# A transformer layer's feed-forward part: four sums per block move from GpSimd to VectorE and read PSUM, raw w2 tiles are fetched two slots ahead, and the last superblock keeps one chain per token tile

## The chip, the cores and the metric

One Trainium2 chip, of which the kernel uses one core. The metric is the device time in microseconds (us) of one execution. TensorE is called PE here, VectorE DVE, ScalarE ACT, GpSimd POOL, and SyncE, which issues nearly all DMAs, SP.

## What is computed

One layer of a transformer with a mixed attention: retention heads beside grouped-query attention, then a feed-forward part whose activation is the square of a relu. The sizes are 2048 tokens of width 1024, and 4096 hidden columns. All is float32 at the kernel's border.

```python
x = x + g1 * (jnp.concatenate([ret, att], axis=-1) @ w_out)

h2 = _modulate(_rmsnorm(x, norm2_g), sh2, sc2)
x = x + g2 * _sqrelu_mlp(h2, w_ff1, w_ff2)
...
def _sqrelu_mlp(h, w1, w2):
    return jnp.square(jax.nn.relu(h @ w1)) @ w2
...
return _rmsnorm(x, final_norm_g)
```

The change touches only the last two lines of the layer: the feed-forward part and its way to the end of the kernel.

## The kernel before, in words

**Number format.** Each float32 operand of a large product is split into two float16 parts, hi and lo. A product of 128 rows of depth then takes three matmuls of 512 columns: hi by hi, hi by lo, lo by hi. A split is two instructions: ACT writes hi as a float16 copy, and DVE subtracts hi from the source to give lo (L66 to L72, `split16`).

**Seven products for eight.** Both feed-forward products are done block-wise by a scheme with seven half-size products and some sums and differences (Strassen-Winograd). Up: a block `b` is 256 hidden columns for one half of the tokens (1024). There are 16 blocks for each half, 32 in all. The seven products of a block are listed in `UP` (L1643): each has a weight part (`a11`, `s1`, ...) made by `sum_w1` on POOL and `form_w1` on ACT and DVE, a part of the activations `hf`, and the name of its PSUM chain, A, B or C. Product n=0 starts chain A, n=1 chain B, n=3 chain C; the others go on accumulating in an open chain. After each product, `up_out` (L1673) takes what it needs from PSUM: ACT copies chain A to tile `v` after n=0, to `q` after n=2, to `w` after n=4 (L1687); DVE adds chain B to `v` after n=1 and chain C to `q` after n=6 (L1678), and chain C to `w` after n=4 (L1699); ACT applies the relu (L1682). So the four quarters of the hidden activations end up in four SBUF tiles: a11 in `v`, a12 in `r`, a21 in `q`, a22 in `w`. They are squared by ACT (L1708).

**The sums of u.** From the squared quarters `sum_r` makes, on POOL, s1 = a21 + a22, s3 = a11 - a21, s2 = s1 - a11, s4 = a12 - s2 (L1713). In the profile these are the four rows of L1713 whose outputs are `s`, `q`, `v` and `r`. The seven tiles a11, a12, a22, s1 to s4 are then split into float16 pairs by `split_r`: the profile calls them `ua` (of `v`, `r`, `w`) and `us` (of `s`, `v`, `q`, `r`).

**Down.** Two blocks make a superblock `s`; there are eight for each half of the tokens, 16 in all. Its seven products are listed in `DOWN` (L1749): each takes one of those seven pairs, one tile `w2t` of w2, and a chain A to D for each of four tiles `m` of 128 tokens (`down`, L1799; PSUM tiles `pd`, four banks). After each, `down_out` (L1813) adds the bank, scaled, to an SBUF tile on DVE (L1824): either to a quarter of an output tile `acc`, or, for n=0 and n=2, to `accu` ("u"), a running sum that three of the four output quarters share. At the end of a half, `add_sum` (L1826) adds `accu` to those three quarters.

**Order.** The instruction order on each engine is written by hand. A unit `g` is one step of the loop at L1972: the four parts of one up product (12 matmuls), `up_out`, and two down products of the superblock before (six matmuls each) with their `down_out`. A block takes 7 units, a superblock 14; there are 224 units, then a tail with the last superblock's 28 down products. Side work is put into units by `at(g, ...)`: the entries with `first=True` run between the first down product and its `down_out`, the others between the second and its own. `rows_of` (L1731) places squares, splits and sums. In units 4 to 13 there is no down product yet.

**Preparing w2.** During the first half of the tokens, 16 jobs (`w2_job`, L1754) each fetch two raw tiles `w2r` of w2, multiply them with a gate row on POOL (L1765), form four differences on POOL (L1551) and seven float16 pairs `w2f` on ACT and DVE (L71, L72), and store the pairs to DRAM. Each job has a slot of five units; fetch stands in the slot's unit 0, gate in 1, forms in 2 to 5. Between the jobs are four slots `h_pair`, which prepare the second half's activations (`hb`, `hs`, `hp`) in a similar way. Job 0 runs in the prelude, interleaved with the last of the attention (`prelude`, L1863); there, the places are counted from `k0`, the end of attention.

**PSUM.** Eight banks: four for up (`pu`, pool `ps1`, handed out in turn) and, from unit 14 on, four for down (`pd`, pool `ps2`).

Of the kernel before, what the change touches and what calls it, by code (L numbers as in the profile page):

```python
# [22 lines left out]
P = 128  # L23
# [32 lines left out]
def layer_kernel(ctx: ExitStack, tc: tile.TileContext, a: dict, out: bass.AP):  # L56
# [1548 lines left out]
    ff = {}  # L1605
# [3 lines left out]
    def open_early():  # L1609
        attn.close()  # L1610
        keep.close()
        ff["h"] = pool(early_ff, "fh", 7)
        ff["w1"] = pool(early_ff, "fw", 7)
        ff["r"] = pool(early_ff, "fr")
        ff["ps1"] = pool(early_ff, "fp1", 4, space=PSUM)

# [39 lines left out]
    pu, rs = {}, {}  # L1656

    def up_part(b, n, k):
        c = UP[n][2]
        first = n in (0, 1, 3)  # L1660
        if k == 0 and first:
            pu[c] = ff["ps1"].tile([P, HALF], F32, name="pu", tag="pu")
        whi, wlo = (w1[b, n][:, x, k] for x in range(2))
        hi, lo = (hs[n][:, x, k] for x in range(2))
        more = {"skip_group_check": not first}
        mm(pu[c], whi, hi, start=first and k == 0, stop=False, **more)  # L1666
        mm(pu[c], whi, lo, start=False, stop=False, **more)  # L1667
        mm(pu[c], wlo, hi, start=False, stop=k == 3, **more)  # L1668

    def new_r(name):  # L1670
        return ff["r"].tile([P, HALF], F32, name=name, tag="r", bufs=8)

    def up_out(b, n):  # L1673
# [6 lines left out]

        def relu(r, src=None):
            nc.scalar.activation(r, r if src is None else src, AF.Relu, scale=scu)  # L1682
            return r
# [5 lines left out]
        if n == 0:  # L1689
            copy("v")  # L1690
        elif n == 1:
            x["a11"] = relu(add(x["v"], x["v"]))
        elif n == 2:
            copy("q")
        elif n == 3:
            x["c"] = ps
        elif n == 4:
            copy("w")
            nc.vector.tensor_tensor(x["w"], x["c"], x["w"], op=ALU.add)  # L1699
            x["a22"] = relu(x["w"])  # L1700
        elif n == 5:
            x["a12"] = relu(new_r("r"), ps)
        elif n == 6:
            x["a21"] = relu(add(x["q"], x["q"]))

# [4 lines left out]
    def sum_r(b, to, x, y, op, at=None):  # L1710
        r = rs[b]
        r[to] = r[at] if at else new_r(to)
        nc.gpsimd.tensor_tensor(r[to], r[x], r[y], op=op)  # L1713

# [16 lines left out]
    def rows_of(b, g):  # L1731
# [5 lines left out]
        at(g + 7, split_r, b, "a12")  # L1737
        at(g + 7, square_r, b, "a21")
        at(g + 7, sum_r, b, "s1", "a21", "a22", ALU.add)
        at(g + 7, sum_r, b, "s3", "a11", "a21", ALU.subtract, "a21")  # L1740
        at(g + 8, sum_r, b, "s2", "s1", "a11", ALU.subtract, "a11")
        at(g + 8, sum_r, b, "s4", "a12", "s2", ALU.subtract, "a12")
        at(g + 8, split_r, b, "s1", first=True)
        at(g + 9, split_r, b, "s2", first=True)
# [9 lines left out]
    def w2_job(b, load, do):  # L1754
# [23 lines left out]
        for i in range(2):  # L1778
            load(0, fetch, i)
            do(1, gate, i)  # L1780
        plan = [(2, "b11"), (2, "b21"), (3, "t2"), (3, "t1"), (4, "b22"), (4, "t3"), (5, "t4")]
        for k, w in plan:
            do(k, form, w)
            load(k + 1, store, w)
        do(2, difference, x, "t1", "b12", "b11")
        do(2, difference, x, "t2", "b22", "t1")
        do(3, difference, x, "t3", "b22", "b12", "b12")
        do(4, difference, x, "t4", "b21", "t2", "t1")

# [7 lines left out]
    accs, pd, sums = [None] * NM, {}, {}  # L1797

    def down(s, n, m):  # L1799
        ua, _, c, _ = DOWN[n]  # L1800
        first = n in (0, 2, 3, 5)
        if first:
            pd[c, m] = ff["ps2"].tile([P, HALF], F32, name="pd", tag="pd")
# [59 lines left out]
    def prelude(k0):  # L1863
# [29 lines left out]
    with tc.manual_schedule():  # L1893
# [20 lines left out]
        for i, job in enumerate(jobs):  # L1914
# [47 lines left out]
        for lo, g0 in ((0, g + 9), (4, g + 13)):  # L1962
# [3 lines left out]
            for m in range(lo, lo + 4):  # L1966
# [130 lines left out]
```

## Time and profile before

| | us |
|---|---|
| time, median of 3 runs | 2908.1 (2907.28 to 2911.85) |
| time of the profiled execution | 2909.34 |
| span of that execution in the profile | 2907.6 |
| PE busy | 2674.7 (92%) |
| DVE busy | 2144.3 (74%) |
| ACT busy | 1569.5 (54%) |
| POOL busy | 1609.6 (55%) |

The profiled execution's time is 1.7 us longer than its span. The profile page gives busy time by engine, groups of instructions by line with the idle time in front of them and what ended it, and a chain of waits; the trace can be asked for groups, waits and the busy time in any stretch. The feed-forward matmuls start at 1578 us of the span, unit 14 (the first with down products) near 1680 us, and the last matmul ends near 2896 us. PEclk is the granted clock of the PE array as a share of full speed.

### The profile page before, as it was taken

The page shows a single profiled execution, that of the slowest core. Times are in us where ns is not written, and L with a number is a line of the kernel's source. Part 1 is how long each engine was busy: PE and PEld are TensorE (multiplying, and loading weights), DVE is VectorE, ACT ScalarE, POOL GpSimd, SP SyncE. Part 2 cuts the span into 40 slices and gives each one's busy share as a digit, 9 for nine tenths or more (in the row PEclk, how much of TensorE's full clock was granted, in tenths as well). Part 3 has the DMA queues.
Part 4 walks back from the last instruction along what each step waited for, and adds up shares of the span by engine and source line. Part 5 has one row for each costly group of instructions (what it writes and reads, how often), then busy time and mean ns, then how long its engine had stood idle before and what let it go on. Part 6 is the DMA issues. An engine that isn't in the chain of part 4 may idle for free.

```text
span 2907.6 us, 44941 instructions
## 1 busy us (share of the span) xinstructions
PE 2674.7 (92%) x16768; PEld 1423.5 (49%) x16768; DVE 2144.3 (74%) x3209; ACT 1569.5 (54%) x2711; POOL 1609.6 (55%) x1275
## 2 busy tenths in 40 slices
PE   7999999988899999999997689889889999999997
PEld 2545644545566666665664234334334444444443
DVE  4856777578877778777774788878798776666666
ACT  3634753247777777777775454444444454444433
POOL 2623762437666668677776766766664443333324
PEclk8999999999999999999999899999999999999999
DMA  7478667552112123232325555544555352222212
GB/s 251 132 254 298 203 203 228 173 187 76 41 61 85 50 82 91 73 97 72 100 62 210 184 175 181 167 151 161 170 169 190 113 195 80 80 80 80 80 51 94
DMA packets 267945, 394.64 MB, mean 136 GB/s; under 512 B 107143, under 2 KB 158343, under 8 KB 265934
## 3 DMA queue, kind: packets, MB, share of 16 engines
q1 hardware_dynamic: 267438, 390.72, 41.5%
q8 instruction: 132, 2.16, 0.3%
q10 hardware_dynamic: 288, 1.05, 0.1%
q14 instruction: 87, 0.71, 0.1%
HBM read 290.87 MB, written 100.82 MB: 135 GB/s over the span
## 4 chain that ended last, share of the span: by engine, by line
PE 61%; DVE 15%; POOL 6%; issue 6%; DMA 6%; ACT 5%; SPq 1%; POOLq 0%; DVEq 0%; ACTq 0%
PE pso L646 5%; PE pso L647 5%; PE pso L648 5%; PE pd L1809 4%; PE pd L1811 4%; PE pd L1810 4%; PE pu L1666 4%; PE pu L1668 4%; PE pu L1667 4%; PE o L239 3%; PE mp L168 3%; PE st L205 3%; PE st L206 3%; DVE w2f L72 2%; DVE plo L224 2%
## 5 line engine op out<-in xcount | busy, mean ns | idle before, releaser
L181 DVE TENSOR_REDUCE nm<-mp 128x1 f32<-128x512 f32 (+1 forms) x576 | 390.3, 685 | 155.0 <-PE mp L168 126.4
L222 POOL TENSOR_TENSOR plo<-p,phi 128x1024 f16<-128x1024 f32 x160 | 353.1, 2208 | 163.8 <-ACT phi L215 135.1
L211 ACT ACTIVATE p<-st 128x512 f32<-128x512 f32 x576 | 338.4, 598 | 180.8 <-PE st L206 108.6
L1666 PE MATMUL pu<-hf,w1f 128*128 128x512 f16 x896 | 346.2, 386 | 41.2 <-ACT w L1687 26.4
L1667 PE MATMUL pu<-hf,w1f 128*128 128x512 f16 x896 | 346.1, 386 | 0.0
L1668 PE MATMUL pu<-hf,w1f 128*128 128x512 f16 x896 | 345.5, 386 | 0.0
L215 ACT ACTIVATE phi<-p 128x1024 f16<-128x1024 f32 x288 | 304.3, 1057 | 0.0
L647 PE MATMUL pso<-wlo,h 128*128 128x512 f16 (+1 forms) x816 | 295.6, 362 | 2.8 <-DVE wlo L544 2.8
L646 PE MATMUL pso<-whi,h 128*128 128x512 f16 (+1 forms) x816 | 295.7, 362 | 1.1 <-ACT whi L543 1.1
L648 PE MATMUL pso<-whi,h 128*128 128x512 f16 (+1 forms) x816 | 295.4, 362 | 0.0
L1713 POOL TENSOR_TENSOR s<-q,w 128x512 f32<-128x512 f32 x32 | 43.3, 1355 | 453.4 <-ACT q L1708 453.4
L224 DVE TENSOR_TENSOR plo<-p,phi 128x512 f16<-128x512 f32 x256 | 243.4, 952 | 15.6 <-ACT phi L215 14.4
L238 PE MATMUL o<-wv,plo 128*128 128x65 f16 x2304 | 235.3, 193 | 18.4 <-POOL plo L222 9.8
L1824 DVE SCALAR_TENSOR_TENSOR acc<-pd,sc,acc 128x512 f32<-128x512 f32 x320 | 234.9, 742 | 11.5 <-PE pd L1811 10.8
L239 PE MATMUL o<-wv,phi 128*128 128x129 f16 x2304 | 243.0, 221 | 0.0
L238 PEld LDWEIGHTS <-plo 128*128 128x128 f16 x2304 | 206.1, 98 | 64.0 <-POOL plo L222 20.8
L1809 PE MATMUL pd<-w2t,us 128*128 128x512 f16 x512 | 196.0, 383 | 41.7 <-DVE acc L1824 39.7
L205 PE MATMUL st<-qr,ks 128*128 128x512 f16 x576 | 220.5, 383 | 14.8 <-ACT p L211 13.3
L206 PE MATMUL st<-qr,ks 128*128 128x512 f16 x576 | 220.7, 383 | 0.1
L239 PEld LDWEIGHTS <-phi 128*128 128x128 f16 x2304 | 205.7, 97 | 21.4 <-issue 0.9
L168 PE MATMUL mp<-ks,qr 128*128 128x512 f16 x512 | 196.3, 383 | 21.5 <-DVE nm L181 21.1
L1810 PE MATMUL pd<-w2t,us 128*128 128x512 f16 x512 | 196.3, 383 | 0.0
(356 smaller groups left out, 6259.9 us busy)
## 6 DMA issues: line engine op xcount, KB each, us to landing
w2t<-w2f SPq DMA_DIRECT2D x112, 512.0 KB, 4.2
wm<-in_w_ff SPq DMA_DIRECT2D x64, 512.0 KB, 5.3
w1r<-in_w_ff SPq DMA_DIRECT2D x64, 512.0 KB, 5.1
w2f<-w2f SPq DMA_DIRECT2D x112, 256.0 KB, 2.2
wmr<-in_w_mod SPq DMA_DIRECT2D x32, 512.0 KB, 5.1
w2r<-in_w_ff SPq DMA_DIRECT2D x32, 512.0 KB, 4.9
hf<-hp SPq DMA_DIRECT2D x56, 256.0 KB, 3.2
hf<-hf SPq DMA_DIRECT2D x14, 1024.0 KB, 6.9
```

The costliest lines, as they stand in the source:

```text
L181: nc.vector.tensor_reduce(dst, src, axis=AX.X, op=ALU.max, negate=True)
L211: nc.scalar.activation(self.p[kt // 2][:, kt % 2], self.s.pop(kt), AF.Exp, scale=HD**-0.5)
L222: nc.gpsimd.tensor_tensor(lo, p, hi, op=ALU.subtract)
L238: mm(o[:, : HD + 1], lo[:, i, c], v[:, : HD + 1], start=False, stop=False)
L239: mm(o, hi[:, i, c], v[:, :VW], start=False, stop=last)
L646: mm(self.ps[:, c], hi[:, k], wh, start=k == 0, stop=False)
L647: mm(self.ps[:, c], hi[:, k], wl, start=False, stop=False)
L648: mm(self.ps[:, c], lo[:, k], wh, start=False, stop=k == KT - 1)
L1666: mm(pu[c], whi, hi, start=first and k == 0, stop=False, **more)
L1667: mm(pu[c], whi, lo, start=False, stop=False, **more)
L1668: mm(pu[c], wlo, hi, start=False, stop=k == 3, **more)
L1810: mm(ps, uh, wl, start=False, stop=False, **more)
```

## The change

Three things are changed.

1. **Sums of u.** `sum_r` runs on DVE. Two of its operands stay in PSUM: a12 stays in chain A's bank and a21 in chain C's bank; relu and square work in the bank, and s1, s3, s4 and the split of a12 read it there. The up pool is laid out anew for that: three banks in turn for chains A and C, and one of its own for chain B (`up_bank`). Bank A is so held until s4 is made, bank C until s3. The sums and splits stand at other places: square a21 first in unit g+7; s1 and s3 first in g+8; s2 and the split of s1 late in g+8; s4 and the split of s2 first in g+9.
2. **w2 jobs.** In each slot fetch stays in unit 0, the gate moves from unit 1 to 2 and all that follows by one unit, so that a job's end overlaps the next job's fetch. In the prelude, job 0's fetch moves from k0+6 to k0-12, its gate from k0+16 to k0+8, and the gate row's fetch from k0+4 to k0-12; its forms stay at k0+20 and after. The steps of `h_pair` after its two fetches move by one unit too.
3. **Last superblock.** Its products go by a list of their own (`LAST`): one chain A per token tile, through n=0, 2, 5, 6, lies in the four up banks, which are idle by then; its partial sums go to the output quarters directly, so that "u" isn't needed. The running sums of the superblocks before are added by POOL in units 220 to 223 in place of the tail. The first three products come in the order n=1, 0, 2, and side work is placed once per down product, not once per two.

```diff
-        ff["ps1"] = pool(early_ff, "fp1", 4, space=PSUM)
+        ff["ps1"] = pool(early_ff, "fp1", 3, space=PSUM)
...
+    def up_bank(c):
+        return ff["ps1"].tile([P, HALF], F32, name="pu", tag="pb" if c == "B" else "pu", bufs=1 if c == "B" else 3)
...
-            pu[c] = ff["ps1"].tile([P, HALF], F32, name="pu", tag="pu")
+            pu[c] = up_bank(c)
...
-            x["a12"] = relu(new_r("r"), ps)
+            x["a12"] = relu(ps)
         elif n == 6:
-            x["a21"] = relu(add(x["q"], x["q"]))
+            x["a21"] = relu(add(ps, x["q"]))
...
-        nc.gpsimd.tensor_tensor(r[to], r[x], r[y], op=op)
+        nc.vector.tensor_tensor(r[to], r[x], r[y], op=op)
...
-        at(g + 7, square_r, b, "a21")
-        at(g + 7, sum_r, b, "s1", "a21", "a22", ALU.add)
-        at(g + 7, sum_r, b, "s3", "a11", "a21", ALU.subtract, "a21")
+        at(g + 7, square_r, b, "a21", first=True)
+        at(g + 8, sum_r, b, "s1", "a21", "a22", ALU.add, first=True)
+        at(g + 8, sum_r, b, "s3", "a11", "a21", ALU.subtract, "q", first=True)
         at(g + 8, sum_r, b, "s2", "s1", "a11", ALU.subtract, "a11")
-        at(g + 8, sum_r, b, "s4", "a12", "s2", ALU.subtract, "a12")
-        at(g + 8, split_r, b, "s1", first=True)
+        at(g + 8, split_r, b, "s1")
+        at(g + 9, sum_r, b, "s4", "a12", "s2", ALU.subtract, first=True)
...
-            do(1, gate, i)
-        plan = [(2, "b11"), (2, "b21"), (3, "t2"), (3, "t1"), (4, "b22"), (4, "t3"), (5, "t4")]
+            do(2, gate, i)
+        plan = [(3, "b11"), (3, "b21"), (4, "t2"), (4, "t1"), (5, "b22"), (5, "t3"), (6, "t4")]
...
+    LAST = [("A", (0, 0)), ("B", (0, 0)), ("A", (0, 1)), ("C", (4, 1)), ("C", (0, 1)), ("A", (4, 1)), ("A", (4, 0))]
+
     def down(s, n, m):
         ua, _, c, _ = DOWN[n]
         first = n in (0, 2, 3, 5)
-        if first:
+        if s == 2 * NS - 1:
+            c, first = LAST[n][0], n in (0, 1, 3)
+        if first and s == 2 * NS - 1 and c == "A":
+            pd[c, m] = up_bank("AAAB"[m])
+        elif first:
             pd[c, m] = ff["ps2"].tile([P, HALF], F32, name="pd", tag="pd")
...
-        on(k0 + 4, "dma", fetch_gate)
-        places = (6, 16, 20, 24, 27, 30, 31)
+        on(k0 - 12, "dma", fetch_gate)
+        places = (-12, None, 8, 20, 24, 27, 30, 31)
...
-                    at(g + (0 if k < 2 else 1 + (k - 2) // 3), step)
+                    at(g + (0 if k < 2 else 2 + (k - 2) // 3), step)
...
+        g = NU * (2 * NS - 1)
+        for i, q in zip((10, 10, 12), ((0, 1), (4, 0), (4, 1))):
+            for m in range(4):
+                at(g + i + m // 2, add_sum, m, q, nc.gpsimd)
...
-        order = [(n, m) for n in range(3) for m in range(4)]
+        order = [(n, m) for n in (1, 0, 2) for m in range(4)]
...
-            if n == 2:
-                for q, eng in zip(QUADS, (nc.vector, nc.gpsimd, nc.gpsimd)):
-                    add_sum(m, q, eng)
-            elif n == 4:
+            if n == 4:
```

How the instructions stand on the engines is shown at two places. The first is DVE's order around up products n=1 and n=2 in the eleventh block of the program, where no w2 form falls between. `v<-pu,v` is the add after n=1, `us` and `w1f` are the subtractions of a split of u and of a w1 part, `accu` and `acc` with `pd` are evictions of down products. Before:

```order
L1678 TENSOR_TENSOR v<-pu,v 128x512
L72 TENSOR_TENSOR us_24150<-s_24113,us_24150 128x512
L1650 SCALAR_TENSOR_TENSOR w1f<-w1r,sc_298,w1f 128x512
L1824 SCALAR_TENSOR_TENSOR accu<-pd,sc_300,accu 128x512 x2
L72 TENSOR_TENSOR us_24199<-v,us_24199 128x512
```

And now:

```order
L1681 TENSOR_TENSOR v<-pu,v 128x512
L1716 TENSOR_TENSOR s_24137<-pu,w 128x512
L1716 TENSOR_TENSOR q<-v,pu 128x512
L1650 SCALAR_TENSOR_TENSOR w1f<-w1r,sc_298,w1f 128x512
L1835 SCALAR_TENSOR_TENSOR accu<-pd,sc_300,accu 128x512
L1716 TENSOR_TENSOR v<-s_24137,v 128x512
L72 TENSOR_TENSOR us_24152<-s_24137,us_24152 128x512
L1835 SCALAR_TENSOR_TENSOR accu<-pd,sc_300,accu 128x512
L1716 TENSOR_TENSOR s_24189<-pu,v 128x512
L72 TENSOR_TENSOR us_24191<-v,us_24191 128x512
```

The four sums of L1716 (s1, s3, s2, s4) stand between the add of n=1 and the evictions of the two units; the split of s1 has moved behind the first eviction.

The second place is POOL's order in the prelude, at the end of the attention: `oo<-oo,ogate` is the last retention tile, `w2r<-w2r,g2b` are job 0's two gates, `cv_f` and `cy_f` the root of a norm, and `xr<-xr,cy_f` that norm, which PE's transposes of the same tile wait for. Before:

```order
L1352 TENSOR_TENSOR oo<-oo,ogate 128x512
L1208 TENSOR_SCALAR cv_f<-ss 128x1
L1209 TENSOR_TENSOR cy_f<-cv_f,half 128x1
L1765 TENSOR_TENSOR w2r<-w2r,g2b 128x1024 x2
L1490 TENSOR_SCALAR xr<-xr,cy_f 128x1024
```

And now:

```order
L1352 TENSOR_TENSOR oo<-oo,ogate 128x512
L1768 TENSOR_TENSOR w2r<-w2r,g2b 128x1024 x2
L1208 TENSOR_SCALAR cv_f<-ss 128x1
L1209 TENSOR_TENSOR cy_f<-cv_f,half 128x1
L1490 TENSOR_SCALAR xr<-xr,cy_f 128x1024
```

The two gates stand ahead of the root now. On SP, the fetches of the gate row and of the two raw w2 tiles, which stood behind the seven fetches of `hf`, stand ahead of them.

More of the change, by code (lines that the diff above doesn't have):

```diff
@@ L1679, in add, with relu @@
             return to
-        def relu(r, src=None):
-            nc.scalar.activation(r, r if src is None else src, AF.Relu, scale=scu)
+        def relu(r):
+            nc.scalar.activation(r, r, AF.Relu, scale=scu)
             return r
@@ L1784, in w2_job @@
             load(k + 1, store, w)
[L1785 to L1788, printed above, removed]
+        do(3, difference, x, "t1", "b12", "b11")
+        do(3, difference, x, "t2", "b22", "t1")
+        do(4, difference, x, "t3", "b22", "b12", "b12")
+        do(5, difference, x, "t4", "b21", "t2", "t1")
     w2 = {}
@@ L1814, in down_out @@
         _, _, c, to = DOWN[n]
+        if s == 2 * NS - 1:
+            c, to = LAST[n]
         ps = pd[c, m]
@@ L1919, in layer_kernel @@
                 for k, step in enumerate(h_pair(1, int(job[1]))):
-                    at(g + (0 if k < 2 else 1 + (k - 2) // 3), step)
-        end_jobs = 4 + 5 * len(jobs) + 2
+                    at(g + (0 if k < 2 else 2 + (k - 2) // 3), step)
+        end_jobs = 4 + 5 * len(jobs) + 4
         for s in range(2 * NS):
@@ L2002, in layer_kernel @@
         for i, (n, m) in enumerate(order):
-            if i % 2 == 0:
-                now(NU * 2 * NS + i // 2, True)
-                now(NU * 2 * NS + i // 2, False)
+            for first in (True, False):
+                now(NU * 2 * NS + i, first)
             down(s, n, m)
             down_out(s, n, m)
-            if n == 2:
-                for q, eng in zip(QUADS, (nc.vector, nc.gpsimd, nc.gpsimd)):
-                    add_sum(m, q, eng)
-            elif n == 4:
+            if n == 4:
                 end_square(1, m)
```

## The prediction

> **What bounds the kernel now.** I read the page's busy shares first, then the busy time by stretch, then the waits of PE and of DVE in the stretch that stood out, and last the groups of that stretch by line. The stretches: prelude, the blocks with w2 jobs, two free blocks, two blocks in which the first half's outputs are finished, twelve blocks of the second half, the end. The columns are the stretch, its length, busy time and count of PE, PEld, DVE, ACT and POOL, the granted PE clock, the DMA share and GB/s.
>
> ```profile
> PE 2674.7 (92%) x16768; PEld 1423.5 (49%) x16768; DVE 2144.3 (74%) x3209; ACT 1569.5 (54%) x2711; POOL 1609.6 (55%) x1275
> ```
>
> ```profile
> 1575.95:1680.30 104.35, 68.03 (x278) 30.03 (x277) 68.42 (x61) 39.65 (x72) 63.17 (x42) 0.84 0.63 234
> 1680.30:2231.80 551.50, 490.81 (x2186) 216.62 (x2184) 451.69 (x498) 261.79 (x459) 367.76 (x228) 0.96 0.50 163
> ...
> 2304.30:2384.70 80.40, 74.44 (x337) 33.12 (x336) 61.90 (x68) 43.78 (x74) 43.08 (x29) 0.98 0.53 177
> 2384.70:2819.80 435.10, 435.10 (x2017) 197.26 (x2016) 296.07 (x374) 176.24 (x300) 138.11 (x97) 1.00 0.24 78
> ```
>
> PE at 92% looks like the bound, and in 2384.7:2819.8 it is: 2017 matmuls in 435.1 us, 0.2157 each, no idle time, so a block of 168 takes 36.2 us. But 1680.3:2231.8 holds 2186 matmuls, 13 blocks, which would take 471.5 at that pace and took 551.5: 80 us too long, 42.4 a block. The two finishing blocks lose 80.4 - 72.7 = 7.7. Now the waits of PE (1570 to 2420) and of DVE (1680.3 to 2231.8): sum, number, longest.
>
> ```profile
> PE pd L1809 <- DVE acc L1824: 40.2, 29, 4.3
> PE pu L1666 <- ACT w L1687: 26.4, 6, 12.0
> PE bank L1495 <- DVE al L1455: 13.0, 1, 13.0
> ```
>
> ```profile
> DVE w1f L1650 <- ACT w1f L1649: 48.4, 32, 4.5
> DVE us L72 <- ACT us L71: 41.6, 20, 6.2
> DVE q L1678 <- PE pu L1668: 3.4, 2, 1.7
> ```
>
> In the 13 blocks DVE is busy for 451.7 and waits 48.4 + 41.6 on ACT, but only 3.4 on PE: with small waits that fills the 551.5. So there the chain of DVE and ACT sets the pace (34.7 busy and 7.7 waiting a block), and PE waits for evictions. Why DVE takes so long is in its groups and POOL's in the same stretch (busy time, mean in ns, idle time ahead and what ended it), and in the least, median and longest durations that the listing of L1650 gives for the whole run:
>
> ```profile
> L72 DVE TENSOR_TENSOR w2f<-w2r,w2f 128x512 f16<-128x512 f32 x54 | 65.2, 1242 | 3.3 <-ACT w2f L71 2.5
> L1650 DVE SCALAR_TENSOR_TENSOR w1f<-w1r,sc,w1f 128x512 f16<-128x512 f32 x40 | 58.7, 1467 | 22.7 <-ACT w1f L1649 22.7
> L1650 DVE SCALAR_TENSOR_TENSOR w1f<-w1s,sc,w1f 128x512 f16<-128x512 f32 x53 | 55.5, 1048 | 25.6 <-ACT w1f L1649 25.6
> ...
> L72 DVE TENSOR_TENSOR w2f<-hs,w2f 128x512 f16<-128x512 f32 x40 | 38.4, 985 | 0.5 <-ACT w2f L71 0.5
> ...
> L72 DVE TENSOR_TENSOR ua<-r,ua 128x512 f16<-128x512 f32 x14 | 16.3, 1166 | 0.3 <-ACT ua L71 0.3
> ```
>
> ```profile
> L1765 POOL TENSOR_TENSOR w2r<-w2r,g2b 128x1024 f32<-128x1024 f32 x26 | 69.4, 2687 | 49.1 <-DMA w2r<-in_w_ff 44.8 <-DVE us L72 4.4
> ...
> L1713 POOL TENSOR_TENSOR q<-v,q 128x512 f32<-128x512 f32 x13 | 20.5, 1573 | 1.0
> L1713 POOL TENSOR_TENSOR s<-q,w 128x512 f32<-128x512 f32 x14 | 20.3, 1451 | 68.5 <-ACT q L1708 68.5
> L1713 POOL TENSOR_TENSOR v<-s,v 128x512 f32<-128x512 f32 x13 | 17.8, 1373 | 0.0
> L1713 POOL TENSOR_TENSOR r<-r,v 128x512 f32<-128x512 f32 x13 | 17.8, 1370 | 1.0
> ```
>
> ```profile
> L1650 DVE SCALAR_TENSOR_TENSOR w1f<-w1s,sc,w1f x128: 736/751/2825, 1577.2 to 2818.5; 128x512 f16<-128x512 f32 x128
> L1650 DVE SCALAR_TENSOR_TENSOR w1f<-w1r,sc,w1f x96: 739/1748/2844, 1571.2 to 2814.1; 128x512 f16<-128x512 f32 x96
> ```
>
> An instruction of the same form takes 739 ns at best and 1467 in the mean: DVE instructions with both operands in SBUF are stretched, and POOL is busy beside them.
>
> **The sums.** The 53 sums leave POOL: 20.5 + 20.3 + 17.8 + 17.8 = 76.4 of its 367.8 us. On DVE their price is that of the nearest rows, an add with one operand in PSUM and, for s2, one with none:
>
> ```profile
> L1678 DVE TENSOR_TENSOR v<-pu,v x32: 674/682/692, 1600.8 to 2822.4; 128x512 f32<-128x512 f32 x32
> ```
>
> ```profile
> L1828 DVE TENSOR_TENSOR acc<-acc,accu x10: 685/984/1753, 2300.6 to 2868.3; 128x512 f32<-128x512 f32 x10
> ```
>
> The first is never stretched (692 at most), the second is (984 median). So 40 x 0.68 + 13 x 0.98 = 40 us more on DVE. [...]
>
> Against that: (a) DVE's waits on ACT for `us` (41.6), which come from sums that POOL makes late, go: a sum is now made on DVE itself, ahead of its split. I leave 6 for the rest: -36. (b) Stretching. The two groups of `w1f` and the two of `w2f` lose 40 x 0.73 + 53 x 0.31, and, with the 0.68 of the uncontended add as the least for `w2f`, 54 x 0.56 + 40 x 0.31: 88 us for 368 us of POOL, 0.24 per us. 76.4 less of POOL gives -18. (Splits of u are stretched too, and not counted in this.) (c) The split of a12 reads PSUM: 14 x (1.17 - 0.68) = -7. Together 40 - 36 - 18 - 7 = -21, between 0 (all waits come back elsewhere) and the 80 to PE's pace.
>
> The bank held longer adds a wait: product n=3 of the next block takes bank A only when s4 is done. On DVE s4 stands behind the eviction that ends unit g+8; PE reaches that n=3 a unit later, 24 x 0.2157 = 5.18 us. Eviction 0.7 and sum 0.7 leave 3.7 us by which DVE may be late. A `pd` bank may be late by nearly two units, so DVE, where PE waits for it now, is later than that. PE will therefore wait at n=3 (for DVE, L1716) in place of `pd`. That costs nothing as long as DVE does not run dry, which its 3.4 us of waiting on PE says is rare. In the blocks where PE sets the pace, the row to use is one block there:
>
> ```profile
> 2496.07 0.69 DVE L1678 TENSOR_TENSOR v<-pu,v 128x512 f32<-128x512 f32 x1 [0.38 <-PE pu L1668]
> ...
> 2499.08 1.75 DVE L1650 SCALAR_TENSOR_TENSOR w1f<-w1r,sc,w1f 128x512 f16<-128x512 f32 x1
> 2500.75 1.40 DVE L1824 SCALAR_TENSOR_TENSOR accu<-pd,sc,accu 128x512 f32<-128x512 f32 x2
> ...
> 2514.33 0.75 DVE L1650 SCALAR_TENSOR_TENSOR w1f<-w1s,sc,w1f 128x512 f16<-128x512 f32 x1 [1.41 <-ACT w1f L1649]
> ```
>
> From the end of product n=1 to the start of n=3 PE has 36 matmuls, 7.8 us. DVE has to do v, s1, s3, w1f, eviction, s2, us, eviction, s4: nine at about 0.7, 6.3 us. The slack of 1.5 holds one stretched instruction (1.75 against 0.74), not two. I put 0.15 a block for the 14 such blocks, +2; if `w1f`, s2 and `us` were all stretched, (3.0 - 1.5) x 14 = +21.
>
> **The w2 jobs.** In the slots, POOL's gates wait 44.8 us for raw tiles and ACT's forms wait behind them. One unit more is 5.2 us and the wait is 44.8 over 13 jobs, 3.4 each, so most of it goes, unless the fetch itself is late: it is now queued in the unit in which the job before reads its raw tiles last, so SP will wait there for DVE, with `w2t` loads and stores behind it. Those are wanted units later. What the gates hold up in the end is DVE's waits for `w1f`: 32 times, where two of 1.41 a block (relu, then copy, on ACT, as in the last row above) would be 37 of the 48.4; of the other 11 I take -6 (0 to -11). The four `h_pair` slots move by a unit: one that now ends just ahead of the `w` copy gets clear of it, another moves onto it; 0, from -8 to +8.
>
> In the prelude:
>
> ```profile
> 1575.95 1.58 SPq L1760 DMA_DIRECT2D w2r<-in_w_ff  x2
> ```
>
> ```profile
> 1583.97 0.19 POOL L1208 TENSOR_SCALAR cv_f<-ss 128x1 f32<-128x1 f32 x1 [5.52 <-DVE ss L1484]
> 1584.24 0.56 POOL L1209 TENSOR_TENSOR cy_f<-cv_f,half 128x1 f32<-128x1 f32 x1
> 1594.21 4.64 POOL L1765 TENSOR_TENSOR w2r<-w2r,g2b 128x1024 f32<-128x1024 f32 x2 [9.40 <-DMA w2r<-in_w_ff]
> 1598.83 1.55 POOL L1490 TENSOR_SCALAR xr<-xr,cy_f 128x1024 f32<-128x1024 f32 x1
> ```
>
> ```profile
> 1596.58 0.63 ACT L71 ACTIVATE w2f<-w2r 128x512 f16<-128x512 f32 x1 [9.99 <-POOL w2r L1765]
> ```
>
> The raw tiles are fetched at 1575.95, behind `hf`, and POOL gets them at 1594.2. POOL stands still, the norm `xr` behind it starts at 1598.8 instead of 1584.8, ACT waits 10.0, and PE waits 13.0 for its transposes. Fetched ahead of `hf`, the tiles are there in time, and the two gates (4.64) fit into the 5.52 that POOL is idle before the root. PE then waits only for a copy and a subtraction to empty the bank, some 2 us: -11. The fetch puts 1.5 MB ahead of `hf`; at the stretch's 234 GB/s that is 6 us of DMA, the most that `hf` can be late. I take -10 for the prelude, from -4 to -14, and -2 for its one block of sums (21/13).
>
> **The finishing blocks** share the mechanism: -2 of 7.7.
>
> **The last superblock.**
>
> ```profile
> 2869.95 0.38 PE L1809 MATMUL pd<-w2t,us 128*128 128x512 f16 x1 [0.96 <-DVE acc L1824]
> ```
>
> This wait, behind the adds of the running sum on DVE, goes: -1. But a12 is the first operand now, and its split stands on DVE behind the last eviction: 0.7 + 0.7, +1.5. The chain of squares, roots and stores at the end is unchanged. +0.5.
>
> Sum: -21 - 6 - 12 - 2 + 2 + 0.5 = -38.5. Against the profiled execution (2909.3, its span and 1.7 around it) 2870.8; it ran 1.2 above the median of 2908.1, so I forecast 2869.
>
> **Rivals.** *DVE drops out of the way*: POOL's relief is worth more than priced, since the splits of u and the blocked ACT copies follow, and PE's pace rules nearly everywhere. -80 - 7.7 - 12: 2808 at the limit, 2835 halfway. For it: 93 of the 551 us are waits, not work. Against: DVE's own work a block stays near 35 us of 36.2. Chance 0.15. *The waits come back*: DVE waits for `w1f` where it waited for `us`; only the prelude stays, -12 + 2.5: 2898. Chance 0.20. *Slower, by the held bank*: PE's stop at n=3 lets DVE catch up and run dry at n=5 and n=6, where it has least to do. The 29 waits for `pd` show DVE up to nearly two units late, 8 us or more, and the new limit is 3.7: up to 4.3 us a block, +56 for 13; with 1 us in each of the 14 later blocks, +14, and -21 - 6 - 12 as before: 2939. It decides from 1.9 us a block on (13 x 1.9 + 14 = 39). Such a stop can also halve the PE clock:
>
> ```profile
> 2042.80:2056.45 13.65, 3.84 (x10) 1.36 (x10) 7.15 (x9) 5.37 (x9) 5.78 (x5) 0.50 0.63 161
> 1739.00:1750.00 11.00, 8.17 (x37) 3.59 (x37) 11.00 (x13) 4.28 (x8) 7.15 (x5) 1.00 0.77 242
> ```
>
> Around the 12.0 us wait the clock is 0.50, around short waits 1.00; one long wait a block in place of several short ones is worse. [...] Chance of this rival 0.11. *Nothing comes of it*, gains and held bank cancelling within 6 us: 0.04. That leaves 0.50 for the forecast's own range, 2850 to 2888.
>
> **Numbers.** 0.2%, about 6 us, is what a measurement of this kernel can tell from no change. Faster 0.50 + 0.15 + 0.20 = 0.85, same 0.04, slower 0.11. The range takes in the forecast, the case in which the waits come back, and the nearer two thirds of the better one: 2822 to 2900.
>
> **What would show it.** Right: L1716 at 0.68 with little stretching; no wait of PE at L1495 or of POOL for `w2r` in the prelude; DVE's waits for `us` under 10; the 13 blocks in about 525 us; POOL near 290 in them; and PE waits at the up product's first matmul for DVE L1716 in place of `pd`. Wrong: DVE idle on PE in the job blocks (held bank), `w1f` waits above 60 (they came back), or the job blocks near 36.3 us each.

## The result, and the profile after

| | before | after |
|---|---|---|
| time, median (lowest to highest) | 2907.69 us, 4 runs (2907.1 to 2911.85) | 2857.41 us, 4 runs (2857.02 to 2858.73) |
| span of the profiled execution | 2907.6 | 2856.9 |
| from the stretch in which the attention ends to unit 14 (1500.6 of before on) | 179.7 | 168.0 |
| the 13 job blocks | 551.5 | 524.5 |
| the two finishing blocks | 80.4 | 72.5 |
| twelve blocks of the second half | 435.1 | 435.1 |
| the end | 87.8 | 88.0 |

The ratio is 0.9825, with a 95% interval of 0.9808 to 0.9842: 50 us less, where 39 were forecast. The stages are cut at the same matmul of PE's order in both traces. First the changed kernel's busy shares:

```profile
PE 2669.2 (93%) x16768; PEld 1423.5 (50%) x16768; DVE 2119.4 (74%) x3333; ACT 1562.7 (55%) x2711; POOL 1408.4 (49%) x1151
```

POOL has 201 us less to do, and DVE, which took the sums over, also has 25 less. Where this happens is in the busy time by stretch (columns as in the prediction: length; PE, PEld, DVE, ACT, POOL; clock; DMA share; GB/s): the prelude, the 13 blocks, the finishing blocks, the twelve blocks.

```profile
1575.12:1664.30 89.18, 68.79 (x278) 30.63 (x277) 55.35 (x59) 35.91 (x65) 55.81 (x38) 0.85 0.61 219
1664.30:2188.80 524.50, 487.10 (x2186) 216.33 (x2185) 457.53 (x554) 261.33 (x463) 288.77 (x179) 0.97 0.55 178
...
2261.30:2333.80 72.50, 72.50 (x337) 32.88 (x336) 59.96 (x75) 43.69 (x74) 32.19 (x21) 1.00 0.57 196
2333.80:2768.90 435.10, 435.10 (x2017) 197.26 (x2016) 278.58 (x421) 174.68 (x300) 57.12 (x45) 1.00 0.24 78
```

In the 13 blocks DVE is busy for 457.5, 5.8 more than before although it does 52 sums more; it stands idle for 67.0 us where it was 99.8. The finishing blocks now run at PE's pace, no idle time left. Next the waits of PE from 1550 to 2360, and those of DVE in the 13 blocks (sum, number, longest):

```profile
PE pu L1669 <- ACT w L1690: 17.4, 5, 5.6
PE pd L1818 <- DVE acc L1835: 13.1, 10, 4.8
PE pu L1669 <- ACT v L1690: 7.4, 2, 5.1
PE pd L1818 <- DVE accu L1835: 6.5, 5, 4.8
PE bank L1495 <- POOL xr L1490: 4.5, 2, 3.4
PE pu L1669 <- DVE q L1716: 4.0, 3, 3.3
PE bank L1495 <- DVE u L1500: 3.3, 2, 2.9
PE bank L1463 <- DVE xr L1470: 2.7, 1, 2.7
```

```profile
DVE w1f L1650 <- ACT w1f L1649: 49.0, 45, 2.4
DVE w L1702 <- ACT w L1690: 7.5, 2, 4.4
DVE w2f L72 <- ACT w2f L71: 6.5, 3, 3.4
...
DVE us L72 <- ACT us L71: 2.1, 1, 2.1
```

DVE's waits for `us` fell from 41.6 to 2.1. PE hardly ever waits for the held bank (L1716: 4.0 in three waits, 3.35 of it in the prelude). PE's longest waits now are for ACT's copy `w`. Last, the durations of the four sums in the whole run (least, median, longest), and the groups of the two w2 forms and of the w1 parts on DVE in the 13 blocks:

```profile
L1716 DVE TENSOR_TENSOR s<-pu,w x32: 673/678/681, 1635.9 to 2803.4; 128x512 f32<-128x512 f32 x32
L1716 DVE TENSOR_TENSOR q<-v,pu x32: 669/676/679, 1636.5 to 2804.0; 128x512 f32<-128x512 f32 x32
L1716 DVE TENSOR_TENSOR v<-s,v x32: 674/681/2181, 1639.0 to 2804.7; 128x512 f32<-128x512 f32 x32
L1716 DVE TENSOR_TENSOR s<-pu,v x32: 671/677/682, 1645.4 to 2806.6; 128x512 f32<-128x512 f32 x32
```

```profile
L1650 DVE SCALAR_TENSOR_TENSOR w1f<-w1s,sc,w1f 128x512 f16<-128x512 f32 x53 | 64.3, 1213 | 27.8 <-ACT w1f L1649 26.4 <-POOL hp L72 1.4
L1650 DVE SCALAR_TENSOR_TENSOR w1f<-w1r,sc,w1f 128x512 f16<-128x512 f32 x40 | 52.2, 1304 | 22.6 <-ACT w1f L1649 22.6
L72 DVE TENSOR_TENSOR w2f<-w2r,w2f 128x512 f16<-128x512 f32 x56 | 47.9, 893 | 3.4 <-ACT w2f L71 3.4
...
L72 DVE TENSOR_TENSOR w2f<-hs,w2f 128x512 f16<-128x512 f32 x42 | 34.4, 842 | 3.1 <-ACT w2f L71 3.1
```

Three sums have an operand in PSUM, and none of their 96 instances is stretched. The one with both operands in SBUF (s2, output `v`) is, up to 2181 ns. The w2 forms became faster (1242 to 893 ns, 985 to 842), the w1 parts made from sums slower (1048 to 1213).

### The profile page after: what moved, and what is told of

Its sections match the earlier page's. It is cut to its first block, busy times and chain, and to the rows that moved or that the text cites. A ratio compares the mean times of both kernels' runs of the same rounds, so it can differ in the third digit from the quotient of the medians.

```text
span 2856.9 us, 44821 instructions
## 1 busy us (share of the span) xinstructions
PE 2669.2 (93%) x16768; PEld 1423.5 (50%) x16768; DVE 2119.4 (74%) x3333; ACT 1562.7 (55%) x2711; POOL 1408.4 (49%) x1151
## 4 chain that ended last, share of the span: by engine, by line
PE 65%; DVE 15%; DMA 6%; ACT 4%; issue 4%; POOL 4%; SPq 0%; POOLq 0%; DVEq 0%; ACTq 0%
PE pso L646 5%; PE pso L647 5%; PE pso L648 5%; PE pd L1818 4%; PE pd L1820 4%; PE pd L1819 4%; PE pu L1669 4%; PE pu L1670 4%; PE pu L1671 4%; PE o L239 3%; PE mp L168 3%; PE st L205 3%; PE st L206 3%; DVE plo L224 2%; DVE w2f L72 2%
## 5 line engine op out<-in xcount | busy, mean ns | idle before, releaser
L168 PE MATMUL mp<-ks,qr 128*128 128x512 f16 x512 | 196.3, 383 | 21.6 <-DVE nm L181 21.2
L239 PEld LDWEIGHTS <-phi 128*128 128x128 f16 x2304 | 205.3, 97 | 21.3 <-issue 0.7
L1650 DVE SCALAR_TENSOR_TENSOR w1f<-w1s,sc,w1f 128x512 f16<-128x512 f32 x128 | 126.7, 992 | 113.8 <-ACT w1f L1649 112.4
L1818 PE MATMUL pd<-w2t,us 128*128 128x512 f16 x496 | 189.1, 381 | 13.0 <-DVE acc L1835 11.6
L1637 POOL TENSOR_TENSOR w1s<-w1r 128x512 f32<-128x512 f32 x64 | 89.3, 1396 | 205.9 <-DVE w1f L1650 166.4
```

What stands on the lines that cost most here:

```text
L239: mm(o, hi[:, i, c], v[:, :VW], start=False, stop=last)
```

## Experiments

The theory after the result: in the job blocks DVE and ACT together set the pace, so whatever takes time out of DVE's work or out of its waits on ACT shows in the end, whether PE, POOL or a transfer caused it. The rival: PE's own long waits (for `w`, for banks) are what counts, and DVE has room. All kernels compute the whole layer. The last three columns are the stages of each profile, in us, cut as above.

| run | median us (runs) | ratio to before, 95% interval | end of attention to unit 14 | 13 blocks | finishing |
|---|---|---|---|---|---|
| before | 2907.69 (4) | | 179.7 | 551.5 | 80.4 |
| after | 2857.41 (4) | 0.9825 (0.9808 to 0.9842) | 168.0 | 524.5 | 72.5 |
| e1_sums | 2863.55 (5) | 0.9847 (0.9834 to 0.9861) | 169.6 | 529.3 | 72.5 |
| e2_w2 | 2911.02 (11) | 1.0014 (1.0005 to 1.0023) | 171.9 | 565.6 | 82.0 |
| e3_prelude | 2904.37 (11) | 0.9984 (0.9976 to 0.9993) | 176.2 | 552.8 | 82.8 |
| e5_sbuf | 2877.38 (4) | 0.9897 (0.9883 to 0.9910) | 166.6 | 542.7 | 73.1 |
| e6_pool | 2891.20 (5) | 0.9948 (0.9935 to 0.9961) | 166.9 | 559.6 | 72.5 |
| e7_hifirst | 2835.41 (4) | 0.9750 (0.9733 to 0.9767) | 165.1 | 506.8 | 72.5 |
| e8_hp3 | 2842.92 (5) | 0.9779 (0.9765 to 0.9793) | 165.0 | 508.7 | 72.5 |
| e9_both | 2821.67 (4) | 0.9704 (0.9690 to 0.9717) | 165.2 | 487.1 | 72.5 |
| e10_w2_hpair0 | 2919.53 (5) | 1.0045 (1.0033 to 1.0058) | 168.3 | 570.5 | 80.4 |
| e11_w1first | 2858.37 (5) | 0.9836 (0.9823 to 0.9850) | 164.9 | 525.6 | 72.5 |
| e12_hpair0 | 2872.38 (4) | 0.9885 (0.9871 to 0.9898) | 166.6 | 539.6 | 72.5 |
| e14_oldslots | 2828.26 (5) | 0.9729 (0.9716 to 0.9743) | 163.3 | 497.3 | 72.5 |

**The sums alone (e1_sums).** The kernel before with part 1 of the change.

```diff
-        nc.gpsimd.tensor_tensor(r[to], r[x], r[y], op=op)
+        nc.vector.tensor_tensor(r[to], r[x], r[y], op=op)
...
-            x["a12"] = relu(new_r("r"), ps)
+            x["a12"] = relu(ps)
...
```

> The kernel before with the first part alone: sums of u on DVE with operands in PSUM. Theory (the sums carry most of it: DVE's waits for `us` go, POOL stretches DVE less): the 13 job blocks lose 21 of 551.5 us, the finishing blocks nearly all of their 7.7, the prelude 2; 2907.7 - 30 = about 2877, DVE's waits for `us` under 10, no wait of PE for L1716's outputs that adds up to more than 5. Rival (the two parts need each other: without the later gates the waits turn up again as waits for `w1f`): 2895 or more, `w1f` waits above 60.

Measured: 44 us less than before, more than the theory gave, and far from the rival (DVE's waits for `w1f` are 53.3, those for `us` 3.3). The busy time by stretch of before (end of attention to unit 14) and then of e1_sums (the same, the 13 blocks, the finishing blocks):

```profile
1500.60:1680.30 179.70, 136.28 (x922) 74.77 (x923) 114.77 (x139) 94.52 (x165) 120.93 (x87) 0.91 0.52 183
```

```profile
1495.70:1665.30 169.60, 134.17 (x923) 74.52 (x924) 106.66 (x140) 93.29 (x162) 111.77 (x81) 0.92 0.50 177
1665.30:2194.60 529.30, 484.23 (x2186) 215.63 (x2185) 455.44 (x552) 260.54 (x461) 287.61 (x180) 0.98 0.54 176
2267.10:2339.60 72.50, 72.50 (x337) 32.88 (x336) 59.94 (x75) 43.69 (x74) 32.21 (x21) 1.00 0.58 196
```

The 13 blocks lose 22.2, as forecast for the sums (21). Another 18 come from the two places at which I had put down 2 each: 10.1 ahead of unit 14, where DVE has 8 us less to do, and 7.9 in the finishing blocks. The remaining 4.9 us of this profile lie in the attention, ahead of everything that is changed.

**The w2 jobs alone (e2_w2), and only their prelude (e3_prelude).** In the slots the gate stands two units behind its fetch now, not one (two units, not two slots as the title has it). In e3 the slots stay as they were; its edit:

```diff
-        on(k0 + 4, "dma", fetch_gate)
-        places = (6, 16, 20, 24, 27, 30, 31)
+        on(k0 - 12, "dma", fetch_gate)
+        places = (-12, 8, 20, 24, 27, 30, 31)
```

> The kernel before with the second part alone: w2 tiles fetched ahead, in the prelude and in the slots. Theory: prelude -10, slots -6: about 2892; POOL no longer waits 44.8 us for raw tiles but DVE still waits about 40 for `us`. Rival (the slots carry most of the gain in the job blocks): -10 - 25, about 2873. Second rival (the slots bring nothing, the wait for raw tiles only moves): 2898.

> The kernel before with only the prelude's half of the second part: job 0's raw tiles and the gate row fetched 18 and 16 steps earlier, gates 8 steps earlier; all slots as before. Theory: PE's wait of 13.0 us at L1495 falls to about 3, -10: 2898. Rival (the 1.5 MB ahead of the activations, and the gates ahead of the root, cost as much as they save): 2905 to 2909. Whether the 4.4 us by which the attention ran shorter in the profile of the changed kernel belong to the change: if so, this kernel reaches its first feed-forward matmul 4 us earlier too.

Measured: the prelude alone gives 4.6 us (0.0016 of 2907), not 10; 2904.4 is just below its rival (2905 to 2909). The whole second part alone gives nothing: 4 us slower, since the 13 blocks get 14 us longer. No rival had that. The profile of e2_w2 over those blocks has POOL's wait for raw tiles down from 44.8 to 29.5, in part as intended, and DVE's waits for `us` at 39.2 as the theory had them, but ACT waits longer for transfers: the first row was 43.9 before, the second wasn't there.

```profile
ACT hp L71 <- DMA hf<-hp: 48.3, 18, 5.0
...
ACT w2f L71 <- DMA w2f<-w2f: 15.0, 3, 8.8
```

The forms of h_pair and every second form of w2 share two buffers `hp`; a form waits until the store ahead of it has left, and behind it on ACT wait the copies that PE and DVE need (for `w`, PE waits 25.6 us in these blocks, 21.6 before, and DVE 8.8 for 2.5). The attention's 4.4 us do not seem to belong to the early fetch: the matmul that starts at 1500.6 in the profile of before starts at 1495.1 to 1499.8 in the others, e1_sums (1495.7) among them, in which nothing ahead of it is changed. With one profile of before, more can't be said.

**Why the prelude gained so little.** POOL's order of time in the changed kernel, then in e1_sums, which has the old prelude (start, length, what it waited for):

```profile
1570.23 1.27 POOL L1637 TENSOR_TENSOR w1s<-w1r 128x512 f32<-128x512 f32 x1 [4.57 <-DMA w1r<-in_w_ff]
...
1579.01 5.55 POOL L1768 TENSOR_TENSOR w2r<-w2r,g2b 128x1024 f32<-128x1024 f32 x2
1585.33 0.19 POOL L1208 TENSOR_SCALAR cv_f<-ss 128x1 f32<-128x1 f32 x1 [0.78 <-DVE ss L1484]
...
1591.56 1.12 POOL L1490 TENSOR_SCALAR xr<-xr,cy_f 128x1024 f32<-128x1024 f32 x1 [5.39 <-DMA x<-xr]
```

```profile
1565.09 1.27 POOL L1637 TENSOR_TENSOR w1s<-w1r 128x512 f32<-128x512 f32 x1
...
1579.04 0.19 POOL L1208 TENSOR_SCALAR cv_f<-ss 128x1 f32<-128x1 f32 x1 [5.51 <-DVE ss L1484]
...
1589.85 4.64 POOL L1768 TENSOR_TENSOR w2r<-w2r,g2b 128x1024 f32<-128x1024 f32 x2 [9.97 <-DMA w2r<-in_w_ff]
1594.48 1.55 POOL L1490 TENSOR_SCALAR xr<-xr,cy_f 128x1024 f32<-128x1024 f32 x1
```

The gates no longer wait for `w2r`. But the early fetch stands ahead of w1's first tiles too, POOL waits 4.57 us for those, the root comes 6.3 us later, and the norm then waits 5.39 for a store that reads the same tile. In all `xr` starts 2.9 us earlier (3.4, as this trace runs 0.5 behind that of e1_sums before the prelude), not the 10 or so that I counted. The root is also late for a reason on DVE: it waits for `ss`, which stands on DVE behind the forms of w1, and these now run beside POOL's sums of w1 and the gates. Four of them, in e1_sums and then in the changed kernel:

```profile
1572.32 3.08 DVE L1650 SCALAR_TENSOR_TENSOR w1f<-w1s,sc,w1f 128x512 f16<-128x512 f32 x3
1575.33 0.74 DVE L1650 SCALAR_TENSOR_TENSOR w1f<-w1r,sc,w1f 128x512 f16<-128x512 f32 x1
```

```profile
1574.80 4.79 DVE L1650 SCALAR_TENSOR_TENSOR w1f<-w1s,sc,w1f 128x512 f16<-128x512 f32 x3 [0.24 <-ACT w1f L1649]
1579.51 2.84 DVE L1650 SCALAR_TENSOR_TENSOR w1f<-w1r,sc,w1f 128x512 f16<-128x512 f32 x1
```

They take 7.6 us for 3.8. One edit tests the wait for the w1 tiles: the same fetches, placed behind those tiles.

```diff
-        on(k0 - 12, "dma", fetch_gate)
-        places = (-12, None, 8, 20, 24, 27, 30, 31)
+        on(k0 - 7, "dma", fetch_gate)
+        places = (-7, None, 8, 20, 24, 27, 30, 31)
```

> The changed kernel with one edit in the prelude: the gate row and job 0's two raw w2 tiles are fetched right behind the first two raw w1 tiles (k0-7), not ahead of them (k0-12); still ahead of the seven fetches of `hf`. Theory (the early w2 fetch pushed the w1 tiles back: POOL waits 4.57 us for them in the changed kernel, and none in the kernel without the w2 part): that wait goes, the root and everything behind it come 3 to 5 us earlier, 2857 - 4 = 2853. Rival (the DMA engines are full there, what one gains the other loses: POOL waits as long for `w2r`): 2855 to 2860.

Measured: the stage gets 3.1 us shorter in the profile, but the time (2858.4) can't be told from 2857.4. The trace shows that the wait for the w1 tiles goes, as the theory has it (POOL starts its first `w1s` without one), but the root comes only 1.0 us earlier (1584.37), not 3 to 5: the gates now start at 1574.63, and three forms of w1 beside them take 7.26 us. The DMA engines that the rival calls full have a share of 1.01 from 1575 to 1592 us of the changed kernel, and of 0.83 in the 15 us ahead.

```profile
1573.46 7.26 DVE L1650 SCALAR_TENSOR_TENSOR w1f<-w1s,sc,w1f 128x512 f16<-128x512 f32 x3
```

**Sums on DVE from SBUF (e5_sbuf).**

```diff
-            x["a12"] = relu(ps)
+            x["a12"] = relu(new_r("r"), ps)
...
-            x["a21"] = relu(add(ps, x["q"]))
+            x["a21"] = relu(add(x["q"], x["q"]))
...
-        at(g + 9, sum_r, b, "s4", "a12", "s2", ALU.subtract, first=True)
+        at(g + 9, sum_r, b, "s4", "a12", "s2", ALU.subtract, "a12", first=True)
```

> The changed kernel with the sums on DVE but every operand in SBUF: the relu of a12 and the sum of a21 write SBUF tiles again, s3 and s4 overwrite their operands. Banks A and C come free early. Theory (DVE's own work counts, an SBUF pair is stretched): 40 sums x (0.98 - 0.68) = 12 and 14 splits of a12 x 0.49 = 7, so 19 more in the 13 blocks: 2857 + 19 = 2876. Rival (DVE has about 49 us of waits for ACT there, which take it up): 2854 to 2861.

Measured: 2877.4, 1.4 us from the theory. Two of the sums in e5_sbuf, and its 13 blocks:

```profile
L1716 DVE TENSOR_TENSOR s<-q,w x32: 674/682/1731, 1634.8 to 2821.8; 128x512 f32<-128x512 f32 x32
L1716 DVE TENSOR_TENSOR q<-v,q x32: 692/693/2724, 1635.5 to 2822.5; 128x512 f32<-128x512 f32 x32
```

```profile
1663.80:2206.50 542.70, 487.69 (x2185) 215.65 (x2184) 477.52 (x554) 263.60 (x463) 299.10 (x180) 0.97 0.53 173
```

DVE has 20.0 us more to do (477.5 for 457.5) and the blocks take 18.2 more: DVE's work counts nearly one to one, though it also waits for 65 us there. The PSUM operand is hardly faster at its best (673 against 674 ns for the first of these sums, 669 against 692 for the second); what it buys is that it wasn't stretched (at most 682 ns in 96 sums, where from SBUF the first goes up to 1731 and the second to 2724).

**POOL's load given back (e6_pool).** Four adds a block into a scratch tile. For the room, the tiles for u go from 8 buffers to 7, as in e8 and e9 below; that was not tried by itself.

```diff
+    def pool_load():
+        j = xp.tile([P, HALF], F32, name="pj", tag="pj", bufs=1)
+        nc.gpsimd.tensor_tensor(j, g2b[0][:, :HALF], g2b[0][:, HALF:], op=ALU.add)
...
+        if 1 <= b <= 13:
+            for k in (7, 7, 8, 8):
+                at(g + k, pool_load)
```

> The changed kernel with POOL given back the work that the sums were, and nothing else: 52 adds of 128x512 float32 into a scratch tile that nobody reads, four a block in the 13 job blocks, at the places where the sums stood before (the tiles for u go from 8 to 7 buffers for the room). Theory (POOL stretches DVE by 0.24 us for each us of its own, and DVE with ACT sets the pace there): 52 x 1.45 x 0.24 = 18, 2857 + 18 = 2875, no new waits of PE at up products. Rival (the stretch falls into DVE's waits): 2854 to 2861. Second rival (POOL itself is in the way, gates and differences come late): +30 or more, with DVE waiting for `w2f`.

The 13 blocks of e6_pool, and the group of the added instructions:

```profile
1665.00:2224.60 559.60, 496.94 (x2185) 218.30 (x2184) 481.83 (x554) 262.22 (x463) 369.86 (x231) 0.95 0.51 167
```

```profile
L1722 POOL TENSOR_TENSOR pj<-g2b 128x512 f32<-128x512 f32 x52 | 81.6, 1568 | 2.0
```

Measured: 34 us slower than the changed kernel, twice the theory's 18; the second rival's size, but not its cause, since DVE doesn't wait longer for `w2f` (5.8 us for 6.5). DVE is busy for 24.3 us more: 0.30 per us of POOL, not 0.24. The other 10.8 are more idle time of DVE, nearly all of it waits for ACT (`us` 8.3 for 2.1, `w1f` 52.2 for 49.0, `w` 9.7 for 7.5).

**What still sets the pace (e7_hifirst, e8_hp3, e9_both).** The first makes ACT's copy of a w1 part ahead of the copy or relu of its unit; the second gives `hp` a third buffer; the third does both.

```diff
-                    at(max(g + n + 1, 4 + n // 2), form_w1, b + 1, n, first=True)
+                    at(max(g + n + 1, 4 + n // 2), form_w1, b + 1, n, first="pre")
+                    at(max(g + n + 1, 4 + n // 2), form_lo, b + 1, n, first=True)
...
+            now(g, "pre")
             up_out(b, n)
```

```diff
-            f = xp.tile([P, 2, 4, P], F16, name="hp", tag="hp", bufs=2)
+            f = xp.tile([P, 2, 4, P], F16, name="hp", tag="hp", bufs=3)
...
-        return ff["r"].tile([P, HALF], F32, name=name, tag="r", bufs=8)
+        return ff["r"].tile([P, HALF], F32, name=name, tag="r", bufs=7)
...
-            f = xp.tile([P, 2, HALF], F16, name="w2f", tag=tag, bufs=2)
+            f = xp.tile([P, 2, HALF], F16, name="w2f", tag=tag, bufs=3 if tag == "hp" else 2)
```

> The changed kernel with one edit: ACT makes the float16 copy of each w1 part ahead of the copy or relu of the same unit, not behind it; DVE's subtraction stays where it is. Theory (in the job blocks the chain of DVE and ACT sets the pace): DVE's 49 us of waits for `w1f` fall under 15 and the 13 blocks get 25 to 35 shorter: 2822 to 2832. Rival (those waits are slack; PE's long waits come from ACT's `w` copies behind `hp`): 2851 to 2861, the 49 us turning up as waits of DVE for PE or for other ACT results.

> The changed kernel with a third buffer for the tiles `hp` that h_pair's forms and half of the w2 forms write (room from the tiles for u, 7 buffers for 8). In the changed kernel ACT waits 29 us for the stores of `hp`, and PE 17.4 us in 5 waits for the ACT copy `w` behind them, with half the clock around them. Theory (each such wait is lost time): PE's waits for `w` fall under 4, 2857 - 13 - 7 of clock = 2837. Rival (DVE's own work is the pace, the time turns up as waits for `pd`): 2850 to 2857.

> The changed kernel with both edits: w1's copy first on ACT, and the third `hp` buffer. Theory: the gains add as long as PE's own pace (13 x 36.3 = 472 for 524.5 us) isn't reached: 2805 to 2820. Rival (one of the two takes the other's place): no better than the better of the two alone.

A row of DVE's waits of e7_hifirst in the 13 blocks, one of ACT's of e8_hp3, and the 13 blocks of e9_both:

```profile
DVE w1f L1653 <- ACT w1f L1649: 8.7, 5, 2.7
```

```profile
ACT hp L71 <- DMA hf<-hp: 13.0, 6, 4.2
```

```profile
1665.00:2152.10 487.10, 475.82 (x2185) 214.51 (x2184) 458.47 (x555) 262.56 (x463) 299.22 (x180) 0.99 0.58 192
```

Measured: 22, 14.5 and 36 us less than the changed kernel. Each theory is right in kind and a little too large, and no rival's time came. In e7, whose profile is of the slowest of its four runs, the waits for `w1f` drop from 49.0 to 8.7, but only 17 of these 40 us leave DVE's idle time (50.3 for 67.0): the rest turns up, as the rival had it, as waits for PE (16.0 for 2.5) and for other results of ACT (26.0 for 16.1). In e8 ACT's waits for `hp` stores drop from 29.2 to 13.0 and PE's waits for `w` in these blocks from 11.5 to none. DVE's waits for `w` (7.5) go with them, so that e8 can't tell the theory from the rival named at the head of this section; e5 and e7 can. The half clock that e8's expectation names stands in the changed kernel's trace behind three of its five waits, those of 4.9 to 5.6 us (0.50 in 1651.0 to 1654.5, 1935.2 to 1938.7 and 2015.8 to 2018.2); behind those of 0.7 and 1.0 us it is 1.00. Together the edits of e7 and e8 add up (17.7 and 15.8 in the blocks alone, 37.4 together) and bring the blocks to 487, 15.6 us above PE's pace. e9_both is the fastest kernel of this study.

**The shifted slots (e10_w2_hpair0, e12_hpair0, e14_oldslots).** h_pair back to its old place, in e2_w2 and in the changed kernel:

```diff
-                    at(g + (0 if k < 2 else 2 + (k - 2) // 3), step)
+                    at(g + (0 if k < 2 else 1 + (k - 2) // 3), step)
```

> The kernel before with the second part (w2 jobs), except that the four h_pair slots keep their old places. The second part alone took 2911.0, its 13 job blocks 14 us more than before in the profile, most of it in the slots behind an h_pair. Theory (the shifted end of an h_pair meets the next job on the two `hp` buffers, and ACT waits for stores): most of the 14 comes back, about 2899. Rival (the later gates and forms themselves cost it): 2908 to 2913.

> The changed kernel with the four h_pair slots back at their old places, nothing else. Theory (as with the second part alone, the shift puts an h_pair's end onto the next job, and costs): 2857 - 8 = 2849 or less. Rival (with POOL relieved the shift costs nothing, or helps as forecast at most by 8): 2855 to 2865.

Measured: both theories fall, and the sign with them: without the shift each is slower, by 8.5 and by 15 us, more than the rivals allow too. The waits of ACT for w2's stores and of DVE for `w1f` in the 13 blocks, of e12_hpair0:

```profile
ACT hp L71 <- DMA w2f<-w2f: 23.6, 6, 6.8
```

```profile
DVE w1f L1650 <- ACT w1f L1649: 72.2, 48, 5.5
```

In the changed kernel they are 5.3 and 49.0. An h_pair that starts while the job ahead of it still has stores under way finds both `hp` buffers taken; the shift is needed as soon as the jobs end later. So the 14 us that e2_w2 loses come with the later gates and forms, not with h_pair, as the rival of e10 had it: its blocks (570.5) are longer still. The last run takes e9_both and undoes the gates' and h_pair's shift together:

```diff
-            do(2, gate, i)
+            do(1, gate, i)
...
-                    at(g + (0 if k < 2 else 2 + (k - 2) // 3), step)
+                    at(g + (0 if k < 2 else 1 + (k - 2) // 3), step)
```

> The fastest kernel so far (w1's copy first on ACT and a third `hp` buffer, 2821.7) with the slots of the second part put back to their old places: gate in unit 1, forms in 2 to 5, h_pair a unit earlier; the prelude keeps its early fetch. Theory (the shift only makes room for transfers, and with DVE and ACT no longer late the job blocks, 487 us against 472 at PE's pace, hardly feel it): 2817 to 2826. Rival (the fetch ahead of the gates is what lets the job blocks run at PE's pace): POOL waits for raw tiles again, 2832 or more. Second rival (as with the second part alone, the later gates cost): under 2812.

Measured: 6.6 us slower than e9_both, between theory and rival; POOL waits 76.8 us for raw tiles there, 52.7 in e9_both. With the sums on DVE the shift is worth 5 us in the blocks of the changed kernel (524.5, e1_sums 529.3) and 10 in those of e9_both (487.1 for 497.3); with the sums on POOL it costs. Why the sign turns isn't settled: ACT's waits for w2's stores, 19.3 us in e2_w2, are as long in the changed kernel (18.2).

## Why the prediction was right, and where not

The time lies inside the range, 11.6 us below the forecast. By the steps:

**The 13 blocks: right in sum, -27.0 for -27,** partly by chance. The sums cost DVE 40.5 (forecast 40; their groups took 14.2 + 8.8 + 8.7 + 8.8), its waits for `us` fell by 39.5 (36), the split of a12 by 7.5 (7). The stretch of `w1f` and `w2f` fell by 19.0 (18): 217.8 us for the four groups before, 198.8 now. That is a sum, too: the two of `w2f` lose 21.3 and one of `w1f` 6.5, the other gains 8.8. Two things were not in it: the other splits of u, 5.5 us less, and the waits. The term "gates off DVE's `w1f` waits, -6" failed: those waits are 49.0 for 48.4, and DVE's waits for `w` and `w2f` rose by 8.5. e7_hifirst shows what they are: ACT's order inside a unit, not late gates. POOL's waits for raw tiles did not go either (64.0 now, 44.8 before). Without the sums POOL waits longer for them (73.3 in e1_sums, with the old slots), and the later gates take off little, since the fetch itself is late now. The prediction had named that condition and put nothing down for it; SP's wait for DVE's forms of the job before, in the 13 blocks, wasn't there before:

```profile
SPq L1763 <- DVE w2f L72: 42.0, 17, 6.5
```

**The split by parts was wrong.** The forecast gave the sums about 25 us and w2 about 16. Alone, the sums give 44 (some 5 of them in the attention) and w2 nothing; on top of the sums, w2 and the last superblock together give 6, and the stage of the latter is as long as before.

**The prelude: -11.7 for -12,** by luck, from other terms. "PE then waits only for a copy and a subtraction, some 2 us" failed: PE's 13.0 became 3.4 + 2.9 at L1495 (the longest wait in each of the two rows) and 2.7 at L1463. I had counted `hf` behind the early fetch but not the w1 tiles, and had put the gates into POOL's idle time without the stretch of DVE's forms of w1 beside them. So the early fetch shortens this stage by 3.5 us alone (e3_prelude), and e1_sums is only 1.6 behind the changed kernel in it, where I had put 10. The -2 for its sums was mis-sized the other way: 10.1 (e1_sums).

**The finishing blocks: -7.9 for -2.** I scaled the gain of a job block (21/13). But these blocks lack only 4 us each to PE's pace, and they had losses of their own, as the waits of DVE in them, before, show:

```profile
DVE w1f L1650 <- ACT w1f L1649: 9.9, 6, 2.6
DVE us L72 <- ACT us L71: 4.3, 2, 3.0
DVE acc L1851 <- POOL cy_e L1209: 3.8, 1, 3.8
```

The wait for POOL's root and those for `us` are gone now; e1_sums shows that it is the sums.

**The held bank: nothing for +2,** so the slower rival fell. "PE will therefore wait at n=3 in place of `pd`" failed: apart from the prelude PE waited 0.7 us for L1716, and in the 13 blocks it went on waiting for `pd` (19.6). Why the bank came free in time was not tried. The blocks at PE's pace took 435.1 before and after.

**The end: +0.2 for +0.5.** Of the 11.6 us below the forecast, about 4 lie in the attention, which isn't changed: chance, as far as the record goes.

Of the rivals, *DVE drops out of the way* came true in the finishing blocks only; in the 13 blocks e5_sbuf and e7_hifirst show DVE and ACT still setting the pace. *The waits come back* fell: the waits for `w1f` stayed at 49.0.

## What to carry to other kernels

Where an engine is called the bound by its busy share, ask in each stage which waits would remain if one instruction got faster; here DVE, with its waits on ACT, paced the stage at 82% busy. Its work counted nearly one to one (18.2 of 20.0 us in e5_sbuf), its waits on ACT for less (17 of 40 us in e7_hifirst), since other waits took the place of those that went. Moving work from POOL to DVE paid twice here: leaving operands in PSUM was worth 20.0 us (e5_sbuf), and 81 us of load given back to POOL cost 33.8 (e6_pool). Where an engine fills double-buffered tiles for stores, look for its waits on DMA before moving the jobs: what stood behind such a wait on ACT came late too (ACT's waits for `hp` stores were 29.2 us in the 13 blocks, PE's for `w` 11.5, and a third buffer was worth 14.5 us in e8_hp3).

## What the runs showed of the hardware

- An add on DVE with one operand in PSUM took 669 to 682 ns (96 sums of the changed kernel); with both in SBUF it took 673 ns at best and up to 2724 (128 sums of e5_sbuf). With 81 us more of POOL in the 13 blocks (e6_pool) the mean of s4, which reads PSUM, stayed at 674 ns, and that of s2, which reads SBUF alone, rose from 1096 to 1375.
- 81 us more of POOL (52 adds of 1.57 us) lengthened DVE's other work by 24.3 us: 0.30 us per us, where the trace of before had suggested 0.24.
- A third buffer of 2 KB a partition was worth 14.5 us, with one tile for u less; that the smaller pool costs nothing was not tried by itself.
